# Three products of a gated linear attention, cut into two row tiles of 64 rows that share two PSUM banks

## The chip, the cores and the metric

The kernel runs on one core of a Trainium2 chip. The metric is the device time of one execution in microseconds (us); the time before is the median of three runs. A core has five engines that work at the same time and meet through semaphores: TensorE (PE, matrix products; PEld is its loading of the stationary operand), VectorE (DVE), ScalarE (ACT), GpSimd (POOL) and SyncE (SP, which issues the transfers). Products land in PSUM, in eight banks of 128 partitions by 512 fp32 columns.

## The reference

Two layers of a decoder trunk on a sequence of 256 tokens of width 1024. Each layer normalises x, projects it, runs three groups of heads and projects back. Groups A (causal attention, 8 heads) and M (attention into 256 memory tokens, 4 heads) are left out of this cut; group B is the chunked gated linear attention (GLA), with 4 heads, key width 32, value width 64:

```python
for l in range(DEPTH):                                   # DEPTH = 2
    h = rms_norm(x, g_pre[l]);  u = h @ w_in[l]          # split into the inputs of groups A, B and M
    log_a = log_sigmoid(rb @ w_gate_up[l] + b_gate_up[l]) / 16
    ob = gla_attention(qb * 32 ** -0.5, kb, vb, log_a)   # 4 heads, chunks of 64 tokens
    ob = rms_norm(ob, g_gla_out[l]) * silu(gb)
    x = x + concat([oa, ob, om]) @ w_out[l]
# gla_attention, written over the whole sequence, b = cumsum(log_a):
# att[i, j] = sum_d q[i, d] * k[j, d] * exp(b[i, d] - b[j, d])   for j <= i;   out = att @ v
```

## The kernel before

The kernel is one instruction stream per engine. The order on each engine is not written by hand: generators describe the work as steps (engine, estimated cost, ready time, priority), and a planner (`Plan`, L48 to L128) picks the next step by its own estimates. Steps of PE carry a mode, the shape of the part of the array that they use ("full", "64", "64r", "32"); the planner holds a step of another mode back a little and charges a change of mode. When an estimate or a mode changes, all later steps may be placed otherwise. The engines then follow that fixed order, each waiting on semaphores where an operand or a buffer is not ready.

PE's main work are the projections, as three fp32r products each (high and low parts): L1000 (256 or 272 columns) and L1007 (two weight blocks side by side, 512 columns). ACT and DVE split the weights into the parts (whi at L406, wlo at L408), evacuate PSUM and do the softmax; POOL does powers (cc at L484) and scalings. Head norms of q and k go L471 (squares, ACT), L475 and L482 (sums ss, DVE), L484 (cc, POOL), L491 (nh, DVE), and then L504 (transposes of nh, PE).

GLA builds its 256 by 256 decayed products in pieces of causal blocks, for all four heads at once: the heads' 32 key rows are stacked on the 128 partitions, and the moving operand (z, or qbd for the diagonal) holds a copy of the queries for each head that is zero outside that head's rows. So one product over 128 rows gives four heads' columns. The pieces, in `gla` (L640):

- far (L681): the second half of the queries against the first half of the keys, one product of 128 by 512 columns into a bank of its own, evacuated into `rect` as one copy of 512 columns;
- neighbour (L688): within each half, the second chunk of 64 against the first, two products on 64 columns of the array each, 256 columns, copied into `ad` as two copies of 64 partitions by 256;
- diagonal (L694): eight blocks of 32 by 32, products on 32 columns of the array, 128 columns, added into `acc` where a mask says so (L705, one instruction of 256 columns);
- the levels between (level_mms, L616 and L623), three in a first call, three in a second, in banks of their own.

These operands are fp32, so that every one of these products shows as two MATMUL instructions in the trace, each half of the time. Copies go through a helper (L258 and L260 ACT, L264 and L266 DVE), by the planner's choice of engine. At the end L734 multiplies the assembled matrix with the values.

Of the kernel before, what the change touches and what calls it, by code (L numbers as in the profile page):

```python
# [16 lines left out]
P = 128  # L17
# [25 lines left out]
C_DIAG = 128 + 80  # L43
# [125 lines left out]
def trunk(ctx, tc, xp_d, w0_d, memT_d, wvr_d, win_d, wmkv_d, wout_d, wup_d, cst_d, nb_d, out_d):  # L169
# [4 lines left out]
    V, S, G, TE = nc.vector, nc.scalar, nc.gpsimd, nc.tensor  # L174
# [26 lines left out]
    rect = att[:, 2]  # L201
    ad = att[:, 0:2].rearrange("p g h t -> p (g h) t")
# [33 lines left out]
    def op(eng, cost, after=0.0, prio=None, table=None, mode="full"):  # L236
        return ("op", [(eng, cost)], after, prio, table, mode)

    def tiled(cost, after, prio=None, mode="64"):
        return op("P", cost, after, prio, None, mode)  # L240

    def vcost(n, rate=1.04):
        return 65 + rate * n
# [7 lines left out]
    def copy(dst, src, n, psum, after, prio=None, scale=None, alts="SV"):  # L251
        costs = {"S": scost(n, psum, 0 if scale is None else 1),
                 "V": vcost(n, 1.04 if psum else 0.52) + (0 if scale is None else 60),
                 "G": gcost(n, True)}
        eng, t = yield ("op", [(e, costs[e]) for e in alts], after, prio, None, "full")
        if eng == "S":
            if scale is None:
                S.activation(dst, src, AF.Copy)  # L258
            else:
                S.activation(dst, src, AF.Copy, scale=scale)  # L260
        elif eng == "G":
            G.tensor_scalar(dst, src, 1.0 if scale is None else scale, 1.0, op0=ALU.mult, op1=ALU.mult)
        elif scale is None:
            V.tensor_copy(dst, src)  # L264
        else:
            V.tensor_scalar(dst, src, scale, None, op0=ALU.mult)  # L266
        return t
# [372 lines left out]
    def gla(l, tq, tk, tb):  # L640
# [35 lines left out]
        ta = yield ("wait", lv[0])  # L676
        z = zs.data[0][2]
        bk, t0 = yield ("acq", banks, 3)
        b7, b6, bl = (x[2] for x in bk)
        t = yield op("P", 860, max(tz, t3, t0))  # L680
        TE.matmul(b7, lhsT=ee[:, 0:2], rhs=z[:, :, 0:P], start=True, stop=True)  # L681
        trect = yield from copy(rect, b7.rearrange("p (h t) -> p h t", h=4), 512, True, t)
        banks.release(bk[0:1], trect)
        p6 = b6[:, :256].rearrange("p (a t) -> p a t", t=64)
        pd = b6[:, 256:512].rearrange("p (g h t) -> p g h t", g=2, h=4)
        t = yield tiled(427, max(tz, t3, t0))
        for g in range(2):
            TE.matmul(p6[64 * g:64 * g + 64], lhsT=ee[:, 2 + g], rhs=z[:, :, P + 64 * g:P + 64 * g + 64],  # L688
                      start=True, stop=True)
        zlp.release(zs.data, t)  # L690
        t = yield tiled(427, max(tq, tk, t0), None, "32")
        for m in range(8):
            c = m % 4
            TE.matmul(pd[32 * c:32 * c + 32, m // 4], lhsT=kf[:, 32 * m:32 * m + 32],  # L694
                      rhs=qbd[:, :, 32 * m:32 * m + 32], start=True, stop=True)
        es, zz = lv[0].data
        tl = yield tiled(870, max(ta, t0), None, "32")
        level_mms(0, es[0][2], zz[0][2], bl)
        elp.release(es, tl)
        zlp.release(zz, tl)  # L700
        t1 = yield from copy(ad[0:64, 0:4, 64:128], p6[0:64], 256, True, t)
        t2 = yield from copy(ad[0:64, 4:8, 64:128], p6[64:128], 256, True, t)
        t64 = max(t1, t2)
        td = yield op("V", vcost(256), t)
        V.copy_predicated(acc, msk[:, None, C_DIAG:C_DIAG + 32].to_broadcast([P, 8, 32]),  # L705
                          pd.rearrange("p g h t -> p (g h) t"))
        banks.release(bk[1:2], max(t64, td))
        for o in (0, 64):
            t32 = yield from copy(ad[o:o + 32, :, o + 32:o + 64],
                                  bl[o:o + 32, :256].rearrange("p (a t) -> p a t", t=32), 256, True, tl)  # L710
# [546 lines left out]
```

## Time and profile before

| | |
|---|---|
| time, median of 3 runs | 278.67 us (278.08 to 278.72) |
| the profiled execution | 279.74 us, span 278.0 us from the first to the last instruction |
| PE | 271.7 us busy, 98% of the span |
| DVE, ACT, POOL | 228.3, 192.6 and 92.6 us busy |
| mean granted TensorE clock | 1.000 |

The span is what the trace shows; the profiled execution's time is 1.7 us longer, for start and end. Layer 0 takes about the first 144 us and layer 1 the rest. The ends of matmuls in the trace are modelled, so distances between starts tell how long PE was taken: in a run of L1007 the starts are 0.23 us apart, while each is shown 0.39 us long.

### The profile page before, as it was taken

What the parts mean: (1) busy time and instruction counts of PE and PEld (TensorE: products, weight loads), DVE (VectorE), ACT (ScalarE), POOL (GpSimd) and SP (SyncE); (2) the same over time, 40 slices, a digit from 0 to 9 for tenths busy, and PEclk for the clock granted to TensorE, in tenths of its full rate; (3) what the DMA queues carried; (4) which work ended last, traced back from release to release, by engine and by line L of the source; (5) the groups of instructions that cost most, each with busy time, mean ns of one, the idle gap of its engine ahead of it and who ended that gap; (6) DMA issues with size and microseconds to landing.
All of it is one profiled execution on the core that took longest, in us unless ns stands there. A gap on an engine that the chain in (4) does not pass through costs nothing.

```text
span 278.0 us, 5780 instructions
## 1 busy us (share of the span) xinstructions
PE 271.7 (98%) x2140; PEld 241.6 (87%) x2140; DVE 228.3 (82%) x571; ACT 192.6 (69%) x429; POOL 92.6 (33%) x109
## 2 busy tenths in 40 slices
PE   8999999989999999999999999999999999999994
PEld 6998887768998998999999886789888788999994
DVE  3999999979897998978899698978797777898621
ACT  5849895856768867958774878756987764976400
POOL 3422285680543470600053408213234630420000
PEclk9999999999999999999999999999999999999999
DMA  6999618270743152444454645228142516160111
GB/s 208 389 371 356 223 20 323 114 295 7 290 166 103 51 185 121 154 155 151 158 167 164 277 152 202 104 77 322 58 153 92 211 45 261 20 252 34 57 57 40
DMA packets 8556, 45.76 MB, mean 165 GB/s; under 512 B 960, under 2 KB 2384, under 8 KB 3536
## 3 DMA queue, kind: packets, MB, share of 16 engines
q1 hardware_dynamic: 8528, 45.39, 44.7%
q8 instruction: 17, 0.28, 0.4%
q14 instruction: 11, 0.09, 0.1%
HBM read 44.34 MB, written 1.05 MB: 163 GB/s over the span
## 4 chain that ended last, share of the span: by engine, by line
PE 78%; DVE 11%; DMA 4%; POOL 2%; ACT 1%; issue 1%; SPq 1%; POOLq 0%
PE bank L1000 45%; PE bank L1007 17%; DVE wlo L408 4%; PE bank L949 4%; PE bank L934 3%; PE bank L882 3%; DMA raw<-memT_dram 3%; PE bank L504 2%; DMA raw<-w_dram 2%; POOL cc L484 1%; PE bank L734 1%; DVE ol L302 1%; DVE sqs L318 1%; DVE ss L475 1%; ACT pe L899 1%
## 5 line engine op out<-in xcount | busy, mean ns | idle before, releaser
L408 DVE TENSOR_TENSOR wlo<-raw,whi 128x512 fp32r<-128x512 f32 (+1 forms) x144 | 97.9, 703 | 13.2 <-ACT whi L406 11.8
L406 ACT ACTIVATE whi<-raw 128x512 fp32r<-128x512 f32 (+1 forms) x144 | 86.2, 624 | 21.8 <-PE bank L1000 7.9
L1000 PE MATMUL bank<-xh,whi 128*128 128x256 f32 x160 | 46.5, 291 | 0.0
L1000 PE MATMUL bank<-xl,whi 128*128 128x256 f32 x160 | 44.6, 279 | 0.0
L1000 PE MATMUL bank<-xh,wlo 128*128 128x256 f32 x160 | 44.6, 279 | 0.0
L919 POOL TENSOR_SCALAR pe<-pe,rc 128x256 f32<-128x256 f32 (+1 forms) x48 | 29.4, 626 | 39.1 <-DVE rc L916 37.6
L1000 PE MATMUL bank<-oh,whi 128*128 128x256 f32 x128 | 36.2, 282 | 0.0
L1000 PE MATMUL bank<-oh,wlo 128*128 128x256 f32 x128 | 36.0, 281 | 0.0
L1000 PE MATMUL bank<-ol,whi 128*128 128x256 f32 x128 | 36.0, 281 | 0.0
L484 POOL TENSOR_TENSOR cc<-ss,nhalf 128x8 f32<-128x8 f32 x12 | 21.5, 1800 | 40.4 <-DVE ss L482 40.4
L1007 PE MATMUL bank<-whi,xh 128*128 128x512 f32 x80 | 33.4, 418 | 0.0
L1000 PEld LDWEIGHTS bank<-xh,whi 128*128 128x128 f32 x160 | 30.2, 189 | 1.6 <-issue 1.4
L1007 PE MATMUL bank<-wlo,xh 128*128 128x512 f32 x80 | 31.4, 392 | 0.0
L1007 PE MATMUL bank<-whi,xl 128*128 128x512 f32 x80 | 31.3, 392 | 0.0
L1000 PEld LDWEIGHTS bank<-xl,whi 128*128 128x128 f32 x160 | 30.1, 188 | 0.1
L1000 PEld LDWEIGHTS bank<-xh,wlo 128*128 128x128 f32 x160 | 30.2, 189 | 0.0
L1000 PE MATMUL bank<-whi,xh 128*128 128x256 f32 (+1 forms) x96 | 28.2, 294 | 0.0
L1000 PE MATMUL bank<-wlo,xh 128*128 128x256 f32 (+1 forms) x96 | 27.4, 285 | 0.3 <-DVE wlo L349 0.3
L1000 PE MATMUL bank<-whi,xl 128*128 128x256 f32 (+1 forms) x96 | 27.0, 282 | 0.0
L1000 PEld LDWEIGHTS bank<-oh,wlo 128*128 128x128 f32 x128 | 24.6, 192 | 0.0
L1000 PEld LDWEIGHTS bank<-oh,whi 128*128 128x128 f32 x128 | 24.0, 188 | 0.2 <-issue 0.2
L1000 PEld LDWEIGHTS bank<-ol,whi 128*128 128x128 f32 x128 | 24.0, 188 | 0.0
(188 smaller groups left out, 609.3 us busy)
## 6 DMA issues: line engine op xcount, KB each, us to landing
raw<-win_dram SPq DMA_DIRECT2D x23, 1024.0 KB, 5.1
raw<-wout_dram SPq DMA_DIRECT2D x8, 1024.0 KB, 4.9
raw<-wmkv_dram SPq DMA_DIRECT2D x4, 1024.0 KB, 4.9
raw<-memT_dram SPq DMA_DIRECT2D x2, 1024.0 KB, 6.1
raw<-wvr_dram SPq DMA_DIRECT2D x1, 1088.0 KB, 5.1
raw<-w_dram SPq DMA_DIRECT2D x4, 264.0 KB, 4.5
raw<-w_dram SPq DMA_DIRECT2D x2, 528.0 KB, 7.1
nb<-nb_dram SPq DMA_DIRECT2D x1, 1024.0 KB, 9.2
```

The costliest lines, as they stand in the source:

```text
L302: V.scalar_tensor_tensor(lo[:, k], src[:, k], col(l, g0 + k), hi[:, k].bitcast(F32), op0=ALU.mult, op1=ALU.subtract)
L318: V.tensor_tensor(sqs, sqs, sq[:, j], op=ALU.add)
L406: S.activation(hi[:, cs], raw[:, cs], AF.Copy)
L408: V.tensor_sub(lo[:, cs], raw[:, cs], hi[:, cs].bitcast(F32))
L484: G.tensor_tensor(c, ss, nhalf, op=ALU.pow)
L504: TE.transpose(ps[:, m, tt * P:tt * P + P], n[:, tt, m * P:m * P + P], ident)
L882: TE.matmul(bk[hh][2][:, a:b], lhsT=x[ds], rhs=y[ds], start=(j == 0), stop=(j == len(prs) - 1))
L919: G.tensor_scalar(pe[:, hh, a:b], pe[:, hh, a:b], rc[:, hh, qt:qt + 1], 1.0, op0=ALU.mult, op1=ALU.mult)
L934: TE.transpose(bk[0][2][:, dst:dst + P], pe[:, hh, src:src + P], ident)
L949: TE.matmul(po[64 * hh:64 * hh + 64, q0:T], lhsT=vv[:, j, c:c + 64], rhs=pt[:, hh, 256 * j:256 * j + T - q0], start=(j == 0), stop=(j == 1))
L1000: TE.matmul(ps, lhsT=a, rhs=b, start=(first and j == 0), stop=(lastk and j == 2))
L1007: TE.matmul(ps, lhsT=a, rhs=b, start=(first and j == 0), stop=(lastk and j == 2))
```

## The change

The far, neighbour and diagonal products are each cut into two products over 64 rows (one pair of heads each, j = 0 and 1), with half the columns. Rows 0 to 63 of the operands go to one half of the array's rows and write the bank bx[0], rows 64 to 127 to the other half and write bx[1]. All three pieces lie in these two banks (columns 0 to 255 far, 256 to 383 neighbour, 384 to 511 diagonal), where far had a bank of its own before and the other two shared one. Far and neighbour are now one step of PE, with mode "64r" and an estimate of 640 ns; the diagonal is its own step with 230. The copies double: two of 256 columns for far, four of 128 for neighbour, two masked ones of 128 for the diagonal. Line numbers behind the change are 13 higher in the new kernel (L1007 is L1020, L705 is L718); far is L685, neighbour L689, the diagonal L702.

```diff
-        b7, b6, bl = (x[2] for x in bk)
-        t = yield op("P", 860, max(tz, t3, t0))
-        TE.matmul(b7, lhsT=ee[:, 0:2], rhs=z[:, :, 0:P], start=True, stop=True)
-        trect = yield from copy(rect, b7.rearrange("p (h t) -> p h t", h=4), 512, True, t)
-        banks.release(bk[0:1], trect)
-        p6 = b6[:, :256].rearrange("p (a t) -> p a t", t=64)
-        pd = b6[:, 256:512].rearrange("p (g h t) -> p g h t", g=2, h=4)
-        t = yield tiled(427, max(tz, t3, t0))
+        bx, bl = [x[2] for x in bk[:2]], bk[2][2]
+        p6 = [x[:, 256:384].rearrange("p (a t) -> p a t", t=64) for x in bx]
+        pd = [x[:, 384:512].rearrange("p (g h t) -> p g h t", g=2, h=2) for x in bx]
+        t = yield tiled(640, max(tz, t3, t0), None, "64r")
+        for j in range(2):
+            r = slice(64 * j, 64 * j + 64)
+            TE.matmul(bx[j][:, 0:256], lhsT=ee[r, 0:2], rhs=z[r, 2 * j:2 * j + 2, 0:P], start=True, stop=True)
         for g in range(2):
-            TE.matmul(p6[64 * g:64 * g + 64], lhsT=ee[:, 2 + g], rhs=z[:, :, P + 64 * g:P + 64 * g + 64],
-                      start=True, stop=True)
+            for j in range(2):
+                r = slice(64 * j, 64 * j + 64)
+                TE.matmul(p6[j][64 * g:64 * g + 64], lhsT=ee[r, 2 + g],
+                          rhs=z[r, 2 * j:2 * j + 2, P + 64 * g:P + 64 * g + 64], start=True, stop=True)
         zlp.release(zs.data, t)
-        t = yield tiled(427, max(tq, tk, t0), None, "32")
+        trect = 0
+        for j in range(2):
+            t1 = yield from copy(rect[:, 2 * j:2 * j + 2], bx[j][:, 0:256].rearrange("p (h t) -> p h t", h=2),
+                                 256, True, t)
+            trect = max(trect, t1)
+        td = yield tiled(230, max(tq, tk, t0), None, "32")
         for m in range(8):
             c = m % 4
-            TE.matmul(pd[32 * c:32 * c + 32, m // 4], lhsT=kf[:, 32 * m:32 * m + 32],
-                      rhs=qbd[:, :, 32 * m:32 * m + 32], start=True, stop=True)
+            for j in range(2):
+                r = slice(64 * j, 64 * j + 64)
+                TE.matmul(pd[j][32 * c:32 * c + 32, m // 4], lhsT=kf[r, 32 * m:32 * m + 32],
+                          rhs=qbd[r, 2 * j:2 * j + 2, 32 * m:32 * m + 32], start=True, stop=True)
...
-        t1 = yield from copy(ad[0:64, 0:4, 64:128], p6[0:64], 256, True, t)
-        t2 = yield from copy(ad[0:64, 4:8, 64:128], p6[64:128], 256, True, t)
...
-        banks.release(bk[1:2], max(t64, td))
+        for j in range(2):
+            for g in range(2):
+                t1 = yield from copy(ad[0:64, 4 * g + 2 * j:4 * g + 2 * j + 2, 64:128], p6[j][64 * g:64 * g + 64],
+                                     128, True, t)
...
+        for j in range(2):
+            td = yield op("V", vcost(128), td)
+            V.copy_predicated(ac[:, :, 2 * j:2 * j + 2],
+                              msk[:, None, None, C_DIAG:C_DIAG + 32].to_broadcast([P, 2, 2, 32]), pd[j])
+        banks.release(bk[0:2], max(t64, td, trect))
```

How the planner places this on PE is seen in layer 1, before:

```order
L681 MATMUL bank_97<-zl_136,ee 128x512
L1007 MATMUL bank_94<-whi,xh 128x512
L1007 MATMUL bank_94<-wlo,xh 128x512
L1007 MATMUL bank_94<-whi,xl 128x512
L688 MATMUL bank_93<-zl_136,ee 64x256 x2
L694 MATMUL bank_93<-qbd,kf 32x128 x8
L616 MATMUL bank_99<-zl_135,el_131 32x128 x4
```

The same place in the changed kernel, from the second half of far on, with the semaphores that an instruction waits for (Activation is ACT, Pool POOL); of the 16 diagonal products, which alternate between the two banks, the first two stand here, and the levels L616 and L623 follow them:

```order
L685 MATMUL bank_97<-zl_136,ee 128x256 [waits Pool_49]
L689 MATMUL bank_95<-zl_136,ee 64x128 [waits DVE_49]
L689 MATMUL bank_97<-zl_136,ee 64x128
L689 MATMUL bank_95<-zl_136,ee 64x128
L689 MATMUL bank_97<-zl_136,ee 64x128
L1020 MATMUL bank_92<-whi,xh 128x512
L1020 MATMUL bank_92<-wlo,xh 128x512
L1020 MATMUL bank_92<-whi,xl 128x512
L702 MATMUL bank_95<-qbd,kf 32x64 [waits Activation_49]
L702 MATMUL bank_97<-qbd,kf 32x64 [waits DVE_49]
```

Neighbour now follows far at once, the diagonal opens the second tiled group, and it waits for the two copies of far's result (one on ACT, one on DVE in layer 1; both on ACT in layer 0, with six instead of three L1020 ahead). In layer 0 the steps behind it move too. On DVE there, before (att are the copies of neighbour and of a level, wz and el level operands, ss the sums of the head norms):

```order
L264 COPY att<-bank_95 64x4x64
L705 COPY_PREDICATED acc<-cst,bank_95 128x256
L595 TENSOR_TENSOR wz_133<-el_132,qf 128x128
L264 COPY att<-bank_97 32x8x32
L595 TENSOR_TENSOR wz_133<-el_132,qf 128x128
L635 COPY_PREDICATED acc<-cst,bank_97 128x8x16
L595 TENSOR_TENSOR wz_133<-el_132,qf 128x128
L635 COPY_PREDICATED acc<-cst,bank_97 128x16x8
L603 TENSOR_TENSOR el_132<-el_132,kf 128x32x4
L408 TENSOR_TENSOR wlo<-raw,whi 128x512 x2
L475 TENSOR_REDUCE ss_694<-sq_104 128x8
```

In the changed kernel, from the same point on:

```order
L264 COPY att<-bank_94 64x2x64
L408 TENSOR_TENSOR wlo<-raw,whi 128x512 x3
L264 COPY att<-bank_94 64x2x64
L475 TENSOR_REDUCE ss_693<-sq_104 128x8
L475 TENSOR_REDUCE ss_699<-sq_103 128x8
L482 TENSOR_TENSOR ss_693<-ss_693,evx_320 128x8
L595 TENSOR_TENSOR wz_133<-el_132,qf 128x128
L482 TENSOR_TENSOR ss_699<-ss_699,evx_320 128x8
L718 COPY_PREDICATED acc<-cst,bank_94 128x2x64
```

The sums of the head norms moved ahead of the masked adds and of the level operands. Later in layer 0, PE's products L949 (group A's probabilities by values) and L882 (group M's logits), which alternated in four groups before (8 MATMULs of L949 in the trace, 12 of L882, and again), stand as one group of 24 of L882 and one of L949. Behind layer 0, PE's order is as before but for the GLA pieces and the next L504, which stands six instead of three L1020 behind the levels.

## Rows read from the trace of the kernel before

**Rows 1.** The page: busy time by engine, and the granted clock in 40 slices.

```profile
PE 271.7 (98%) x2140; PEld 241.6 (87%) x2140; DVE 228.3 (82%) x571; ACT 192.6 (69%) x429; POOL 92.6 (33%) x109
...
PEclk9999999999999999999999999999999999999999
```

**Rows 2.** Waits of PE: waiting line <- releaser: us in total, times, longest.

```profile
PE bank L504 <- DVE nh L491: 0.8, 2, 0.6
```

**Rows 3.** Timeline of PE, layer 0, the first head-norm transposes: start us, shown length, instruction.

```profile
60.98 0.40 PE L1007 MATMUL bank<-whi,ol 128*128 128x512 f32 x1
61.94 0.33 PE L504 MATMUL bank<-cst,nh 128*128 128x128 f32 x1 [0.56 <-DVE nh L491]
62.47 0.55 PE L504 MATMUL bank<-cst,nh 128*128 128x128 f32 x3 [0.20 <-DVE nh L491]
62.77 0.48 PE L1007 MATMUL bank<-whi,oh 128*128 128x512 f32 x1
```

**Rows 4.** Timeline of PE, layer 1, around GLA's first products.

```profile
170.54 0.39 PE L1007 MATMUL bank<-whi,xl 128*128 128x512 f32 x1
170.76 1.10 PE L681 MATMUL bank<-zl,ee 128*128 128x512 f32 x2
...
172.16 0.40 PE L1007 MATMUL bank<-whi,xl 128*128 128x512 f32 x1
172.49 0.65 PE L688 MATMUL bank<-zl,ee 128*64 128x256 f32 x4
173.07 0.65 PE L694 MATMUL bank<-qbd,kf 128*32 128x128 f32 x16
173.53 0.49 PE L616 MATMUL bank<-zl,el 128*32 128x128 f32 x5
...
174.52 0.51 PE L1007 MATMUL bank<-whi,xh 128*128 128x512 f32 x1
174.86 0.40 PE L1007 MATMUL bank<-wlo,xh 128*128 128x512 f32 x1
```

**Rows 5.** Timeline of PE, layer 0, far's product.

```profile
47.90 1.02 PE L681 MATMUL bank<-zl,ee 128*128 128x512 f32 x2
```

**Rows 6.** Timeline of PE, layer 1, products over 64 rows in two row halves.

```profile
197.35 0.72 PE L882 MATMUL bank<-kfT,qfT 64*128 64x128 f32 x8
197.82 0.37 PE L882 MATMUL bank<-kh,qh 64*128 64x256 f32 x2
```

**Rows 7.** Timeline of PE, window 180.690 to 180.715 us alone.

```profile
180.69 0.26 PE L623 MATMUL bank<-zl,el 128*32 128x64 f32 x4
```

**Rows 8.** ACT: timeline of layer 0, and a group by form (count, busy, mean ns).

```profile
49.12 1.14 ACT L406 ACTIVATE whi<-raw 128x512 fp32r<-128x512 f32 x2
...
L471 ACT ACTIVATE sq<-bank 128x256 f32<-128x256 f32 x16 | 5.4, 373 | 1.9 <-PE bank L1007 1.8
```

**Rows 9.** DVE: timeline of layer 1, and a group by form.

```profile
172.27 0.28 DVE L585 TENSOR_TENSOR el<-b 128x128 f32<-128x128 f32 x1
174.27 0.42 DVE L491 TENSOR_TENSOR nh<-bank,cc 128x256 f32<-128x256 f32 x1
...
L460 DVE COPY R<-bank 128x256 f32<-128x256 f32 x2 | 0.8, 418 | 0.2 <-PE bank L457 0.2
```

**Rows 10.** The chain that ended last, layer 0: start us, us, what.

```profile
51.80 0.60 DVE wlo L408
...
56.97 1.19 DVE ss L475 x2
...
58.32 3.12 POOL cc L484
```

**Rows 11.** The chain that ended last, groups M and A in layer 0.

```profile
88.14 0.80 PE bank L949 x8
88.94 0.91 PE bank L882 x12
...
118.73 1.45 PE bank L949 x16
```

More of the change, by code (lines that the diff above doesn't have):

```diff
@@ L700, in gla @@
         zlp.release(zz, tl)
-        t1 = yield from copy(ad[0:64, 0:4, 64:128], p6[0:64], 256, True, t)
-        t2 = yield from copy(ad[0:64, 4:8, 64:128], p6[64:128], 256, True, t)
[L703 to L706, printed above, removed]
-        banks.release(bk[1:2], max(t64, td))
+        t64 = t
+        for j in range(2):
+            for g in range(2):
+                t1 = yield from copy(ad[0:64, 4 * g + 2 * j:4 * g + 2 * j + 2, 64:128], p6[j][64 * g:64 * g + 64],
+                                     128, True, t)
+                t64 = max(t64, t1)
+        ac = acc.rearrange("p (g h) t -> p g h t", g=2)
+        for j in range(2):
[3 more added lines that the diff above has]
+        banks.release(bk[0:2], max(t64, td, trect))
         for o in (0, 64):
```

## The prediction

> **What bounds the kernel now.** I read the page first. PE is busy in 98% of the span, and the granted clock stands at its upper level in all 40 slices [rows 1]. Busy matmuls say little by themselves, since their ends are modelled, so I went through PE's timeline and compared distances between starts: 0.23 us in a run of L1007. Next I read PE's waits. After the start-up the largest entry is L504, which waits for nh on DVE [rows 2], and the timeline shows where: in layer 0, near 61 us [rows 3]. The last L1007 starts at 60.98 and is through at 61.21; L504 starts at 61.94, 0.73 late, and its second product 0.53 behind the first where 0.11 is the pace, another 0.42. PE stands for 1.15 us there. So PE's work is the bound nearly everywhere: work that PE saves shows in the time one to one, a new wait of PE costs one to one, and DVE, ACT and POOL count only where PE waits for them.
>
> **The products themselves.** The place to price is layer 1 [rows 4]. From 170.77 (L1007 at 170.54 and its 0.23) to the second L1007 behind the levels at 174.86 there are 4.09 us, with four L1007 of 0.23 in them: 3.17 us of GLA. Its parts: far 0.86 by layer 0's pace, where the next L1007 is held back accordingly [rows 5]; neighbour 172.49 to 173.07, 0.58; diagonal to 173.53, 0.46. Into a tiled group costs 0.10 (172.16 to 172.49 is 0.33 and not 0.23). Out of one costs about 0.22: 174.52 to 174.86 is 0.11 over the pace, and I take as much before it.
>
> What half the rows and half the columns do is shown by L882, which already works on 64 rows in pairs [rows 6]: eight MATMULs of 128 columns take 0.47 us. Far's 0.43 for each MATMUL of 512 columns makes 0.107 for 128; eight in a row would be 0.86, four pairs side by side 0.43. So pairs run side by side. The first round is late by some 0.10 (0.47 less 0.43, and what the first pair needs before the second starts; this is an estimate).
>
> - Far: 0.43, with the first round 0.53 (bounds 0.43 and, with no overlap, 0.86).
> - Neighbour: four tiles at once, 0.21, and 0.10 for the change of tile shape that 0.58 against 0.43 shows today: 0.31 (0.21 to 0.86).
> - Diagonal: 32 MATMULs of half the columns of today's 16. With eight tiles at once 0.23; with issue at today's 0.46/16 = 29 ns each it would be 0.92. The nearest row is L623, products of the same 64 columns: four start inside a window of 25 ns [rows 7], about 7 ns apart, so 32 need some 0.22. I take 0.25, and 0.10 for the change of shape to the levels.
> - The levels stay: 173.53 to 174.52 and 0.11, 1.10.
> - Far becomes tiled, so there is one more pair of in (0.10) and out (0.20 to 0.22).
>
> Sum: 0.10 + 0.53 + 0.31 + 0.20 for the first group, 0.10 + 0.25 + 0.10 + 1.10 for the second, 2.69 against 3.17. I take 0.45 saved in a layer, **0.9 us in both**. This is little, because the second way in and out takes back 0.3.
>
> The Trainium skill, "TensorEngine Tiling (Array Packing)", Instruction Overhead, says that a matmul costs about 60 cycles however few columns it has, and warns against tiling a dimension that is small already. At 2.4 GHz that is an estimate of 25 ns, 0.80 us for the diagonal and 1.1 us more over both layers. The trace disagrees with it for tiles side by side, by the four starts in 25 ns.
>
> **The new wait.** The diagonal now writes banks that ACT and DVE still read, and the order shows L702 waiting for both copies of far. In layer 0 both stand on ACT. PE starts far at 47.90 [rows 5]; with 1.15 for the group, six L1007 (1.38) and 0.10, L702 could start at 50.5. ACT has L406 at 49.12 [rows 8], the first copy at 49.64, another L406 and then the second copy. L406 takes 0.52 from start to start (1.14 for two, each 0.62), a copy of 256 columns like L471's 0.37, with the next 0.29 behind its start. The second copy ends at 49.64 + 0.29 + 0.52 + 0.37 = 50.82. With 0.06 for the semaphore, **0.35 lost**. In layer 1 the second copy is DVE's, behind L585 at 172.27 [rows 9], so 172.47 to 172.89; PE would be ready at 170.77 + 1.14 + 3 x 0.23 = 172.60. **0.3 lost.** Bounds: none where the queues run early, one L406 (0.52) or L408 (0.60) more each where they run late. What stands behind L702 on PE is everything: levels, projections. So the products' 0.9 shrinks to 0.25.
>
> On DVE in layer 1 four small copies wait for L702 (to about 173.4) and stand ahead of both L491, the second of which starts at 174.27 today [rows 9] and would end near 175.85. L504 moved back by three L1007, to about 175.77: **0.1 to 0.15 lost** (0 to 0.6).
>
> The added copies (six instructions a layer, at some 0.2 to 0.3) are about 0.8 us of ACT and DVE. They are hidden as long as PE is the bound; uncovered they would cost that much.
>
> **What moves in layer 0.** The head-norm sums L475 start at 56.97, 5.17 us behind the L408 at 51.80 [rows 10], after the masked adds and level operands that the order shows there. In the new order that L408 comes one place earlier, at about 51.1, and only four L408 (0.60 each) and two small copies (0.2) lead from there to the sums: L475 near 53.9, cc near 55.3 and, with the 3.12 that this first cc takes, done near 58.4. DVE comes to L491 at about 58.0, so nh is whole near 59.2. PE's next L504 stands behind 30 L1007, which begin at 50.85 + 0.25 + 0.10 + 1.10 = 52.3, so at 59.2. Its wait of 1.15 would go; I take **1.0**, since both sides meet within 0.1 (0 to 1.15).
>
> Later in layer 0, L949, L882, L949, L882 [rows 11] take 0.80 + 0.91 + 0.80 + 0.91 = 3.42. As one group of 24 L882 (12 pairs at 0.12 and 0.20 for the first, 1.6) and 16 L949 (1.45 as the same row group shows) they take 3.05: **0.4 saved** (0 to 0.5).
>
> **Sum.** -0.9 + 0.65 + 0.15 - 1.0 - 0.4 = -1.5 us. The profiled execution took 279.74 us, 0.4% over the median; its span of 278.0 becomes 276.5, and the median 278.67 - 1.5 = **277.2 us**.
>
> **The rivals.**
> - The wait of L504 stays (18%). cc's 3.12 us is one reading, and DVE's and ACT's queues ahead of L491 are estimates that meet PE within 0.1 us. Then layer 0 gains nothing up to 62 us, layer 1 nets zero, and the 0.4 of the merged groups is left: 278.3, no measurable change.
> - The copies come later than I read them (10%): one more L406 in layer 0 and L408 in layer 1 ahead of them, 1.1 more: 278.3. For it speaks that ACT and DVE have little idle time there; against it, that the order puts one instruction between the result and the later copy. The Trainium skill says the like in the same page, PSUM Bottleneck: tiling speeds up TensorE and not the evacuation, which can become the bound; the wait in the order agrees, no run here shows its length yet.
> - The diagonal is bound by issue (9%): 0.92 for 0.25, 1.35 in both layers: 278.5. By the page's 25 ns it would be 278.3.
> - The row halves do not run side by side (7%), so the same columns pass twice: far 0.86, neighbour 0.86, diagonal 0.92, together 1.55 more a layer: 280.3, slower. L882 speaks against it, where the halves also write two banks. It turns the result to slower from 1.2 us more in a layer on.
>
> **The numbers.** Under 0.3% (0.84 us) a measurement of this kernel hardly tells from no change. Faster is the forecast alone, 56%, with a range of its own from 276.4 (all of its terms at their good end without the copies' wait would be near 276) to 277.8. Within 0.3% lie the first three rivals, 37%; slower is the last, 7%. To leave out no more than 2 in 10, the range must take in the first three: 276.4 to 278.6.
>
> **What would show it.** Right: L685 and L689 as one group of about 1.1 us; the 32 MATMULs of L702 within 0.3; a stop of PE of 0.3 to 0.4 ahead of L702 in either layer, put down to ACT's and DVE's copies; no stop ahead of L504 in layer 0; one L882 group of 24. Wrong: a gap ahead of L504 near 60 us that is still about 1 us; L702 at 0.9; a copy of far that ends more than 0.5 behind PE; new stops of PE in the attention part of layer 0, where the order changed most and which I priced at nothing.

## The result, and the profile after

The changed kernel takes 276.6 us (median of 6 runs, 276.46 to 277.49; the kernel before on the same chip 278.7). The ratio is 0.9911, with a 95% interval of 0.9889 to 0.9933: 2.5 us less (278.67 x 0.0089), where I forecast 1.5. The direction was right, the size was not: by the ratio the time is 276.2, just below my range. The two profiled executions differ by more, 278.0 against 274.9 us of span.

The page after (busy time, the granted clock in 40 slices), which answers to [rows 1]:

```profile
PE 269.3 (98%) x2184; PEld 240.0 (87%) x2184; DVE 226.5 (82%) x573; ACT 195.2 (71%) x437; POOL 88.6 (32%) x107
...
PEclk9999999999999999999999999999999999999999
```

PE is still the bound, at the same clock. Its timeline at the places of [rows 4, 5], GLA's products in layer 0, and then, as in [rows 3], the first head-norm transposes:

```profile
47.70 0.40 PE L1020 MATMUL bank<-whi,xl 128*128 128x512 f32 x1
48.02 0.70 PE L685 MATMUL bank<-zl,ee 64*128 64x256 f32 x4
48.66 0.45 PE L689 MATMUL bank<-zl,ee 64*64 64x128 f32 x8
49.04 0.50 PE L1020 MATMUL bank<-whi,xh 128*128 128x512 f32 x1
...
50.30 0.39 PE L1020 MATMUL bank<-whi,xl 128*128 128x512 f32 x1
50.62 0.70 PE L702 MATMUL bank<-qbd,kf 64*32 64x64 f32 x32
51.24 0.51 PE L616 MATMUL bank<-zl,el 128*32 128x128 f32 x5
...
52.59 0.40 PE L1020 MATMUL bank<-wlo,oh 128*128 128x512 f32 x1
...
59.01 0.39 PE L1020 MATMUL bank<-whi,ol 128*128 128x512 f32 x1
59.24 0.60 PE L504 MATMUL bank<-cst,nh 128*128 128x128 f32 x4
59.59 0.48 PE L1020 MATMUL bank<-whi,oh 128*128 128x512 f32 x1
```

From the end of the L1020 at 47.70 (its 0.23 gives 47.93) to 52.59 there are 4.66 us with seven L1020 of 0.23 in them, so 3.05 us of GLA. The same count in the kernel before (47.90 to its second L1007 behind the levels at 51.93, less four) gives 3.11. GLA brought 0.06 us here, its new wait included, where I had 0.10 (0.45 less 0.35). At 59.24 L504 follows its predecessor by 0.23: the stop of [rows 3] is not there. In layer 1 the timeline shows a new stop, shorter than that one:

```profile
167.22 0.39 PE L1020 MATMUL bank<-whi,xl 128*128 128x512 f32 x1
167.54 0.70 PE L685 MATMUL bank<-zl,ee 64*128 64x256 f32 x4
168.18 0.45 PE L689 MATMUL bank<-zl,ee 64*64 64x128 f32 x8
...
169.46 0.62 PE L702 MATMUL bank<-qbd,kf 64*32 64x64 f32 x32
170.01 0.51 PE L616 MATMUL bank<-zl,el 128*32 128x128 f32 x5
...
171.35 0.39 PE L1020 MATMUL bank<-wlo,xh 128*128 128x512 f32 x1
...
172.53 0.33 PE L504 MATMUL bank<-cst,nh 128*128 128x128 f32 x1
173.06 0.55 PE L504 MATMUL bank<-cst,nh 128*128 128x128 f32 x3 [0.20 <-DVE nh L491]
173.36 0.48 PE L1020 MATMUL bank<-whi,xh 128*128 128x512 f32 x1
```

GLA takes 2.98 us (167.45 to 171.35, less four L1020) for 3.17; L504 then needs 0.83 up to the next L1020, where four such transposes without a wait take 0.35 (59.24 to 59.59).

What I had nothing for stands in the windows. Of the kernel before and then of the changed one: us, PE busy and its instructions (those that reach in from the edges counted), granted clock, DMA share, GB/s.

```profile
97.20:148.30 51.10, 51.10 (x443) 1.00 0.48 166
124.60:138.60 14.00, 14.00 (x122) 1.00 0.49 168
250.00:270.00 20.00, 20.00 (x172) 1.00 0.13 47
```

```profile
95.00:145.00 50.00, 50.00 (x443) 1.00 0.47 168
122.60:136.60 14.00, 14.00 (x126) 1.00 0.46 174
250.00:270.00 20.00, 20.00 (x172) 1.00 0.12 42
```

The same 443 instructions take 51.1 us in one trace and 50.0 in the other, with no wait of PE for another engine in the view of waits there and the full clock in both. In the 14 us of layer 0's output projection 126 MATMULs fit instead of 122: the starts of L1000 (L1013) with 256 columns lie 117.8 ns apart in one and 113.3 in the other. Both paces occur in each trace; they hold over dozens of products and change where the stream changes: where another instruction or a stop comes between, or where the operands change sides. At 91.66 us of the changed kernel's trace, `whi,xh` becomes `xh,whi` in L1013 with nothing between, and 117.8 becomes 113.3 within three products. In the last 20 us both kernels run at 117.8.

### The profile page after: what moved, and what is told of

Same layout as the page of the kernel before. It is cut to its first block, busy times and chain, and to the rows that moved or that the text cites. A ratio compares the mean times of both kernels' runs of the same rounds, so it can differ in the third digit from the quotient of the medians.

```text
span 274.9 us, 5873 instructions
## 1 busy us (share of the span) xinstructions
PE 269.3 (98%) x2184; PEld 240.0 (87%) x2184; DVE 226.5 (82%) x573; ACT 195.2 (71%) x437; POOL 88.6 (32%) x107
## 3 DMA queue, kind: packets, MB, share of 16 engines
HBM read 44.34 MB, written 1.05 MB: 165 GB/s over the span
## 4 chain that ended last, share of the span: by engine, by line
PE 86%; DVE 5%; DMA 4%; issue 1%; POOL 1%; SPq 1%; ACT 1%; POOLq 0%; DVEq 0%
PE bank L1013 48%; PE bank L1020 21%; PE bank L962 4%; PE bank L947 3%; PE bank L895 3%; DMA raw<-memT_dram 2%; PE bank L504 2%; DMA xp<-xp_dram 2%; DVE wlo L408 1%; POOL oh L262 1%; PE bank L747 1%; DVE sqs L318 1%; DVE ol L302 1%; PE bank L623 1%; PE bank L702 0%
## 5 line engine op out<-in xcount | busy, mean ns | idle before, releaser
L408 DVE TENSOR_TENSOR wlo<-raw,whi 128x512 fp32r<-128x512 f32 (+1 forms) x144 | 97.4, 699 | 13.5 <-ACT whi L406 12.1
L1013 PE MATMUL bank<-xh,whi 128*128 128x256 f32 x160 | 46.3, 289 | 0.0
L1013 PE MATMUL bank<-xl,whi 128*128 128x256 f32 x160 | 44.5, 278 | 0.0
L1013 PE MATMUL bank<-xh,wlo 128*128 128x256 f32 x160 | 44.5, 278 | 0.0
L932 POOL TENSOR_SCALAR pe<-pe,rc 128x256 f32<-128x256 f32 (+1 forms) x48 | 27.3, 583 | 39.9 <-DVE rc L929 27.0
L1013 PE MATMUL bank<-oh,whi 128*128 128x256 f32 x128 | 35.9, 280 | 0.0
L1013 PE MATMUL bank<-ol,whi 128*128 128x256 f32 x128 | 35.8, 280 | 0.0
L1013 PE MATMUL bank<-oh,wlo 128*128 128x256 f32 x128 | 35.7, 279 | 0.0
L484 POOL TENSOR_TENSOR cc<-ss,nhalf 128x8 f32<-128x8 f32 x12 | 20.9, 1746 | 42.0 <-DVE ss L482 35.2
L1020 PE MATMUL bank<-whi,xh 128*128 128x512 f32 x80 | 32.7, 409 | 0.0
L1013 PEld LDWEIGHTS bank<-xh,whi 128*128 128x128 f32 x160 | 30.1, 188 | 1.6 <-issue 1.4
L1020 PE MATMUL bank<-wlo,xh 128*128 128x512 f32 x80 | 31.4, 393 | 0.0
L1020 PE MATMUL bank<-whi,xl 128*128 128x512 f32 x80 | 31.3, 391 | 0.0
L1013 PEld LDWEIGHTS bank<-xl,whi 128*128 128x128 f32 x160 | 30.1, 188 | 0.1
L1013 PEld LDWEIGHTS bank<-xh,wlo 128*128 128x128 f32 x160 | 30.2, 189 | 0.0
L1013 PE MATMUL bank<-whi,xh 128*128 128x256 f32 (+1 forms) x96 | 28.1, 293 | 0.0
L1013 PE MATMUL bank<-wlo,xh 128*128 128x256 f32 (+1 forms) x96 | 27.6, 287 | 0.4 <-DVE wlo L349 0.3
L1013 PE MATMUL bank<-whi,xl 128*128 128x256 f32 (+1 forms) x96 | 27.1, 282 | 0.0
L1013 PEld LDWEIGHTS bank<-oh,wlo 128*128 128x128 f32 x128 | 24.3, 190 | 0.0
L1013 PEld LDWEIGHTS bank<-oh,whi 128*128 128x128 f32 x128 | 24.0, 188 | 0.2 <-issue 0.2
L1013 PEld LDWEIGHTS bank<-ol,whi 128*128 128x128 f32 x128 | 24.0, 188 | 0.1
```

Source lines behind the costliest of these rows:

```text
L408: V.tensor_sub(lo[:, cs], raw[:, cs], hi[:, cs].bitcast(F32))
L484: G.tensor_tensor(c, ss, nhalf, op=ALU.pow)
L932: G.tensor_scalar(pe[:, hh, a:b], pe[:, hh, a:b], rc[:, hh, qt:qt + 1], 1.0, op0=ALU.mult, op1=ALU.mult)
L1013: TE.matmul(ps, lhsT=a, rhs=b, start=(first and j == 0), stop=(lastk and j == 2))
L1020: TE.matmul(ps, lhsT=a, rhs=b, start=(first and j == 0), stop=(lastk and j == 2))
```

## The experiments

All ratios are against the kernel before, with 95% intervals; the changed kernel has 0.9911.

**Each kernel once more.** No edit.

> The kernel before, unchanged, in a second profiled execution. In its first one the 443 matmuls between 97.2 and 148.3 us took 51.10 us, and the same work of the changed kernel 50.0; the L1000 start 117.8 ns apart there against 113.3. If the order of the instructions decides on the pace (A), the same stretch takes 51.0 to 51.2 again and the execution 279.4 to 279.9 us. If the pace is a matter of the single execution (B), it comes out anywhere from 50.0 to 51.1, and the execution between 277.9 and 279.8 us, as the six times of this kernel lie.

> The changed kernel, unchanged, in a second profiled execution. Pace by the order (A): the stretch from 95 to 145 us takes 50.0 us again, 276.7 in all. Pace by the execution (B): up to 1.1 us more in that stretch, 276.5 to 277.8 in all; then about 1.1 of the 3.1 us between the two first profiles says nothing of the change.

The kernel before took 277.96 us (span 276.2), the changed one 276.08 (274.3). In the changed kernel both traces show the same pace nearly everywhere. In the kernel before, the second execution has no stop ahead of L504: POOL's first cc (L484) took 1.67 us, not the 3.1 of the first. Its source view, and the timeline:

```profile
L484 POOL TENSOR_TENSOR cc<-ss,nhalf x2: 1633/1651/1669, 58.0 to 59.7; 128x8 f32<-128x8 f32 x2
```

```profile
60.77 0.39 PE L1007 MATMUL bank<-whi,ol 128*128 128x512 f32 x1
61.00 0.60 PE L504 MATMUL bank<-cst,nh 128*128 128x128 f32 x4
61.36 0.48 PE L1007 MATMUL bank<-whi,oh 128*128 128x512 f32 x1
```

And from 124.6 to 138.6 us it holds 126 MATMULs:

```profile
124.60:138.60 14.00, 14.00 (x126) 1.00 0.42 151
```

So the same program, instruction for instruction, has the stop or has it not (1.15 us), and has the slow or the fast pace there; B is right for the kernel before. But this second execution is a fast one: its 277.96 us lie below all eleven other times of the kernel on that chip (278.63 to 280.01), so most executions pay a part of these losses.

Two smaller stops are in both traces of the kernel before and in neither of the changed one. The second call of the levels waits within its group for el, and L749, the second of a pair of products (L748, L749; L761 and L762 behind the change), waits for qsl. Before, and then after:

```profile
58.68 1.12 PE L623 MATMUL bank<-zl,el 128*32 128x64 f32 x48
59.73 0.50 PE L1007 MATMUL bank<-whi,oh 128*128 128x512 f32 x1
...
80.93 0.19 PEld L749 LDWEIGHTS bank<-qsl,blk 128*128 128x128 f32 x1 [0.34 <-DVE qsl L746]
```

```profile
60.47 0.88 PE L623 MATMUL bank<-zl,el 128*32 128x64 f32 x48
61.27 0.50 PE L1020 MATMUL bank<-whi,oh 128*128 128x512 f32 x1
```

The levels take 1.05 us there (1.11 in the second trace) and 0.80 after the change. The two pairs of L748 and L749 in layer 0 take 0.88 us up to the next starts (1.06 in the second trace) and 0.48 after it. Together these stops cost 0.65 and 0.88 us.

**Order alone, tiles alone.** One kernel has the order of the changed one on every engine with the old products in its places, the other the old order with the tiles:

```diff
# order alone, in gla of the changed kernel
+        TE.matmul(bx[0], lhsT=ee[:, 0:2], rhs=z[:, :, 0:P], start=True, stop=True)
+            TE.matmul(p6[64 * g:64 * g + 64], lhsT=ee[:, 2 + g], rhs=z[:, :, P + 64 * g:P + 64 * g + 64], ...)
...
+            TE.matmul(pd[32 * c:32 * c + 32, m // 4], lhsT=kf[:, 32 * m:32 * m + 32], rhs=qbd[:, :, 32 * m:32 * m + 32], ...)
# tiles alone, in gla of the kernel before: its estimates stay
         t = yield op("P", 860, max(tz, t3, t0))
+        for j in range(2):
+            r = slice(64 * j, 64 * j + 64)
+            TE.matmul(bx[j][:, 0:256], lhsT=ee[r, 0:2], rhs=z[r, 2 * j:2 * j + 2, 0:P], start=True, stop=True)
```

> The order of the changed kernel, instruction by instruction on every engine, but with the products of the kernel before in its places: far as one product of 512 columns, the neighbours of 256, the diagonal of 128, all on 128 rows. If the change of order brings the gain (my reading of the two traces: products 0.06 in layer 0 and 0.2 in layer 1, all else from the order), it is 2.0 to 2.5 us under the kernel before, within 0.5 us of the changed one, and L504 does not wait near 60 us. If the tiles bring it, it stays within 0.5 us of the kernel before.

> The tiles of the changed kernel in the order of the kernel before: the same sequence on every engine, each full product replaced by its row tiles, each copy by its halves. If the order brings the gain (A), this is no faster than the kernel before. By the lengths read in the changed kernel (0.64 far, 0.38 neighbour, 0.55 diagonal, 1.12 levels, 0.09 in) a layer takes 2.78 us for 3.11 to 3.17, 0.7 saved in both; but far and diagonal now follow each other directly, so L702 must wait for far's two copies, 0.5 to 1.0 in a layer: +0.3 to +1.3 us over the kernel before, with the L504 wait near 61 us as there. If the tiles bring the gain (B), it lies 1.5 to 2.5 us under the kernel before.

Order alone: 277.46 us, ratio 0.9933 (0.9914 to 0.9951), 1.9 us less. Tiles alone: 278.87, ratio 0.9988 (0.9979 to 0.9997), 0.3 less, where I had expected 0.3 to 1.3 more. Three quarters of the gain come without a single row tile; L504 is on time in layer 0 (59.32, 0.23 behind the L1020 ahead of it), and the two smaller stops are gone (0.81 and 0.47 us). The other 0.6 are the tiles in the new order: GLA takes 3.32 and 3.38 us with the old products in it, 3.05 and 2.98 with the tiles. In the old order the shared banks bring the wait that I feared, at the neighbour's product in layer 0:

```profile
50.31 0.71 PE L694 MATMUL bank<-zl,ee 64*64 64x128 f32 x8 [0.98 <-ACT att L689]
50.95 0.45 PE L702 MATMUL bank<-qbd,kf 64*32 64x64 f32 x32
51.34 0.52 PE L616 MATMUL bank<-zl,el 128*32 128x128 f32 x5
```

(L694 and L689 are its lines of the neighbour's product and of far's copies.) In layer 1, with the same three L1020 between, no product waits, since ACT comes to the copies earlier, and GLA takes 2.80 us (170.13 to 173.85, less four L1020) for 3.17. The 0.3 us of this run are not the tiles' worth alone: by the 0.98 that PE loses in layer 0 the stops behind it become shorter (no wait at L504 near 61 us, the levels 0.81). In the new order the neighbour's product follows far before any copy reads the banks, and six L1020 (three in layer 1) stand ahead of the diagonal; what is left of the wait is read below. The diagonal, already inside its group and not waiting, takes 0.39 here, change to the levels included. From 124.6 to 138.6 us this kernel holds 121 MATMULs, the order-alone kernel 126 from 122.6 to 136.6.

**The diagonal.** Each of its products twice; and, in the order of the changed kernel, on 128 rows.

```diff
-        for m in range(8):
+        for m in list(range(8)) * 2:                      # twice
...
-            for j in range(2):                            # on 128 rows, one bank for each g
-                r = slice(64 * j, 64 * j + 64)
-                TE.matmul(pd[j][32 * c:32 * c + 32, m // 4], lhsT=kf[r, 32 * m:32 * m + 32], ...)
+            TE.matmul(pd[m // 4][32 * c:32 * c + 32], lhsT=kf[:, 32 * m:32 * m + 32], rhs=qbd[:, :, 32 * m:32 * m + 32], ...)
```

> The changed kernel with every product of the diagonal (L702) issued twice, into the same place. If the group of 32 MATMULs takes its 0.55 to 0.62 us because each costs some 17 to 19 ns to issue (C), 64 take 1.1 to 1.2, and the kernel loses 1.1 us over both layers. If 32 take 0.25, as I forecast, and the rest is a wait for the copies of far that the weight loads hide (D), 64 take 0.80 to 0.87, and it loses 0.5 us.

> The changed kernel, in exactly its order, with the diagonal alone as eight products on 128 rows (16 MATMULs of 128 columns) as in the kernel before, each half in one of the two shared banks. If L702 takes its 0.55 to 0.62 us because of its number of small products (C), this group takes the 0.46 us of before, and the kernel is 0.2 to 0.3 us faster than the changed one. If L702 is held by the copies of far (D), the group still takes 0.55 to 0.62 or starts that much later, and the time is unchanged.

Twice (277.05 us, 0.9924, 0.9901 to 0.9946), in layers 0 and 1:

```profile
50.17 1.09 PE L702 MATMUL bank<-qbd,kf 64*32 64x64 f32 x64
51.19 0.52 PE L616 MATMUL bank<-zl,el 128*32 128x128 f32 x5
...
169.34 0.95 PE L702 MATMUL bank<-qbd,kf 64*32 64x64 f32 x64
170.22 0.52 PE L616 MATMUL bank<-zl,el 128*32 128x128 f32 x5
```

64 take 1.02 and 0.88 us where 32 took 0.62 and 0.55: 32 more cost 0.40 and 0.33, between C and D. The starts of the single MATMULs in the changed kernel settle it. First, in either layer, the later of far's two copies, and what PE has started of L702 by 0.05 us behind that copy's end (windows 50.60 to 50.86 and 169.45 to 169.62 us). Then the run of the tiles in the old order, where all 32 start in a window of 0.25 us (172.11 to 172.36):

```profile
50.45 0.36 ACT L258 ACTIVATE att<-bank 128x256 f32<-128x256 f32 x1
50.62 0.30 PE L702 MATMUL bank<-qbd,kf 64*32 64x64 f32 x2
169.16 0.41 DVE L264 COPY att<-bank 128x256 f32<-128x256 f32 x1
169.46 0.30 PE L702 MATMUL bank<-qbd,kf 64*32 64x64 f32 x2
```

```profile
172.12 0.45 PE L702 MATMUL bank<-qbd,kf 64*32 64x64 f32 x32
```

Two MATMULs, the first product, have started by then. The third, the first to write the bank of the later copy, starts at 50.86 and 169.63, 0.05 to 0.06 behind that copy's end. From it to the last are 0.24 us, 8 ns from start to start, and 0.15 more to L616. So in this kernel 32 take what I forecast. The rest of the 0.62 and 0.55 is a wait for the copy (D), 0.16 and 0.08, and 0.08 between the first two starts, which no run here explains. With the products twice, the first 32 stand 8 ns apart as well; only the second 32, into the same places, take about 0.39 us, 12 ns each.

On 128 rows the group takes 0.49 and 0.46 (L700 at 50.64 to L616 at 51.13; 169.63 to 170.09). That is the time that C named, but it does not speak for C: in this edit the second bank is first written by the fifth product, at 50.89, when the copy is done anyway. The kernel is no faster: 0.9916 (0.9902 to 0.9930). Its trace gains 0.15 us on the changed one at the diagonal of layer 0 and has lost it at 63 us, where L504 takes longer. It is 0.34 ahead from 83 us on, since its products from 70 to 77 us go at 113.3 ns for 117.8. It falls 0.17 behind at layer 1's statistics, where DVE waits 0.90 for whi at 142.7, and ends 0.05 ahead. The diagonal's gain, 0.1% of the time, can't be told from that.

**The pace.** Small extra products at six places of layer 1's output projection; then one transpose ahead of it; then two on the kernel before.

```diff
+                    if (l, g, m) in ((1, 0, 0),) and k == KORD[l][0]:      # before: ((0, 1, 0), (1, 0, 0))
+                        TE.transpose(ps[:, 0:P], ident, ident)
                     mms(ps, l, "f", w, (oh, ol), k, m, k == KORD[l][0], k == KORD[l][-1])
```

> The changed kernel, with a small extra product ahead of each of the six last half groups of the output projection of layer 1 (24 MATMULs of 256 columns each, all at 117.8 ns from start to start so far): a transpose, an fp32r product of 128 columns, two of 256, one of 64 rows, four of 32 columns, two of 64 columns. If the pace is a state that an interruption leaves behind and that holds to the next one (C), some of the six turn 117.8 into 113.3 for the 24 MATMULs behind them, each such piece 0.11 us shorter. If the pace belongs to the place (the banks, the operands, the weights in memory) (D), all six pieces stay at 117.8. The extra products cost 0.1 to 0.4 us each.

> The changed kernel with one extra transpose of 128 x 128 ahead of the output projection of layer 1, near 247 us, into a bank that the next product overwrites. If PE's pace is a state (C), the 192 MATMULs behind it run at 113.3 ns for 117.8: 0.86 us less, 0.11 for the transpose, 0.75 in all: 275.8 us or 1.2% under the kernel before. If the pace does not hold, or something else than PE sets the end (D), the time is that of the changed kernel or 0.1 more.

> The kernel before, without tiles or new order, with two such transposes: one ahead of the second group of the output projection of layer 0 (144 MATMULs behind it) and one ahead of that of layer 1 (192). If the pace is a state that any kernel can set (C): 0.75 less behind the second; behind the first 0.54 less in executions that stood at 117.8 there and 0.1 more in those at 113.3: 0.7 to 1.3 us under the kernel before, and in the profile the stretch from 122 to 142 us at 113.3. Then the drift of 1.1 us between the two first profiles has nothing to do with row tiles. If it hangs on the tiles or on the order (D), no change.

The six pieces, mean distance of starts from the third product on, worked out from the trace: 117.8 ns ahead of the first, then 114.2 behind the transpose, 114.4 (fp32r of 128 columns), 117.8 (two of 256), 113.5 (64 rows), 113.6 (32 columns), 113.5 (64 columns). C is right: with the same operands the pace is what the interruption leaves, and two products of the same width turn it from fast to slow. One transpose in the changed kernel: 275.63 us, 0.9872 (0.9852 to 0.9892), 1.0 us less than the changed kernel by the medians. Its trace gains 0.7 us behind the transpose. Another 0.36 lie far ahead of it: from 70 to 77 us, where the instructions on every engine are the same, it goes at 113.3 ns and the two traces of the changed kernel at 117.8. Two in the kernel before: 278.41, 0.9968 (0.9952 to 0.9983), 0.9 us less with nothing else changed. The windows of the changed kernel with one, then of the kernel before with two:

```profile
250.00:270.00 20.00, 20.00 (x177) 1.00 0.13 47
```

```profile
124.60:138.60 14.00, 14.00 (x126) 1.00 0.41 152
250.00:270.00 20.00, 20.00 (x178) 1.00 0.12 41
```

172 became 177 and 178. So the drift of 1.1 us between my first two traces is a pace of PE that a kernel of either kind can have.

**Layer 1's transposes, and sums of steps.** The four small copies of layer 1 on ACT; that with the transpose; the diagonal on 128 rows with both and two more transposes in layer 0 and layer 1; and far held back until the levels are ready.

```diff
-                t1 = yield from copy(ad[...], p6[j][64 * g:64 * g + 64], 128, True, t)
+                t1 = yield from copy(ad[...], p6[j][64 * g:64 * g + 64], 128, True, t, alts="SS" if l else "SV")
...
-        t = yield tiled(640, max(tz, t3, t0), None, "64r")
+        t = yield tiled(640, max(tz, t3, t0, ta), None, "64r")      # far held back, with the diagonal on 128 rows
```

> The changed kernel, with the four small copies of the neighbour's products in layer 1 given to ACT alone; on PE the order stays, on DVE L491 moves ahead of the place of the four copies. If these copies on DVE (1.19 us ahead of L491) make L504 late in layer 1, 0.49 us by the comparison with the kernel before, that stop near 172.5 us goes, and the kernel is 0.4 to 0.5 us faster than the changed one: 276.1 us. If L504 is late for another reason (the cc of POOL, or nothing but the row before it), it stays late and the time within 0.1.

> The changed kernel with the small copies of layer 1 on ACT and the one transpose ahead of the output projection of layer 1. If the two steps add (0.49 and 0.61 in their profiles), it lies 1.1 us under the changed kernel: 275.0 to 275.4 us, 1.4 to 1.5% under the kernel before. If the pace is thrown by the first step, 276.0.

> The changed kernel with the diagonal on 128 rows, the small copies of layer 1 on ACT, and three transposes (ahead of the second half of qm in layer 0, of qm in layer 1, of the output projection of layer 1). Sum of the steps as read so far: 0.25 + 0.45 + 0.75, and 0.1 to 0.3 each from the first two transposes if the pace holds over the short groups that follow: 1.5 to 1.9 us under the changed kernel, 274.7 to 275.1 us, 1.4 to 1.6% under the kernel before. If the steps don't add, 275.5 or more.

> The changed kernel with two edits: far and neighbour wait in the plan for the operands of the levels, so that they stand closer to the second group, and the diagonal is eight products on 128 rows again, of 128 columns, one bank for each half of them. Where all is one group, a layer's products take 0.09 + 0.64 + 0.38 + 0.46 + 1.12 = 2.69 us for 2.99 to 3.05 in the changed kernel, 0.6 to 0.7 less in both; where the groups stay apart only the diagonal's 0.1 to 0.15 a layer. The order moves with it, so the waits of L504 can come or go: 275.3 to 276.3 without a new one, 276.6 to 277.5 with one near 1 us.

Copies on ACT: 276.13 us, 0.9897 (0.9875 to 0.9919), and L504 is on time:

```profile
171.86 0.60 PE L504 MATMUL bank<-cst,nh 128*128 128x128 f32 x4
172.21 0.48 PE L1020 MATMUL bank<-whi,xh 128*128 128x512 f32 x1
```

0.35 us for the 0.83 of the changed kernel, so the copies on DVE ahead of L491 had cost 0.48. With the transpose the two steps add: 274.89 us, 0.9868 (0.9845 to 0.9892), the fastest version here, 1.7 us under the changed kernel by the medians and 1.2 by the ratios; 0.48 and 0.7 make 1.2, and its profile has the fast pace from 70 to 77 us, too. All steps together gave only 276.01, 0.9889 (0.9869 to 0.9909): the extra transpose in layer 0 met a stretch that stood at 113.3 and left it at 117.8, so it is no switch to the fast pace, and layer 1's statistics cost this trace 0.4 us, as they cost the run with the diagonal on 128 rows 0.5. Far held back: 278.33, 0.9968 (0.9955 to 0.9981), slower than either case that I had expected. The groups did not become one (twelve L1020 stand between them in layer 0), the order moved everywhere behind, and L1020 and L457 wait 0.6 us in new places; where the rest of its loss lies I did not trace.

**The wait of L504, timed by itself.** On the kernel before, two L408 were put behind the two sums L475, alone and with the two transposes. In a first form of the edit the loads overwrote weights before L408 had read them; its times (283.55 and 282.75 us) say nothing. In the mended form:

> The kernel before with one change of order on DVE: the two L408 of layer 0 that stand ahead of the two head-norm sums L475 near 55.4 us come behind them, and the buffers that they read are given back 1.2 us later, so two loads of weights start that much later. The sums end 1.1 us earlier, and L504 near 61 us is no longer late, whether POOL's cc takes 3.1 us or 1.67. If that wait is there in most timed executions (A), the median falls by 0.8 to 1.1 us against the kernel before; if it was a matter of few executions (B), by less than 0.4. If the later loads make PE wait behind 61 us, the profile shows L1007 or L1000 waiting for wlo there.

> The same with the two transposes of the earlier run on the kernel before (0.9 us by that run's ratio). If wait and pace are separate terms that add: 0.9 and what the sums give, 1.3 to 2.0 us under the kernel before. If they are the same executions (an execution that waits loses its pace, too), no more than 0.9 to 1.1.

Both are slower: 281.12 us, 1.0062 (1.0039 to 1.0085), and 280.26, 1.0036 (1.0023 to 1.0049). L482, which closes the sums, still stands behind the two L408, so cc starts at 58.5, no earlier than in the kernel before (58.3); and the later loads make the second pair of L504 wait:

```profile
65.41 0.33 PE L511 MATMUL bank<-cst,nh 128*128 128x128 f32 x1 [0.60 <-DVE nh L498]
66.13 0.55 PE L511 MATMUL bank<-cst,nh 128*128 128x128 f32 x3 [0.39 <-DVE nh L498]
```

(L511 is L504 there.) The edit was no test of the wait, and neither A nor B is decided by it. The transposes take back about 0.9 here, too (281.12 - 280.26), but in the trace only that of layer 1 does: behind that of layer 0 the products stay at 117.8, where the same transpose on the kernel before left 113.3.

## Why the prediction was right and wrong

- **The products**: net right, by luck. I had 0.9 saved and 0.65 lost to the new wait, 0.25 in all; GLA took 0.06 and 0.19 less, 0.25 in all, but by two errors of 0.4 that cancel. Without its waits (0.16 and 0.08 by the starts of L702) GLA saved 0.49: far took 0.64 (forecast 0.53), neighbour 0.38 (0.31), the change of shape behind the diagonal 0.15 (0.10), and I had nothing for the 0.08 between the diagonal's first two starts. The reading of [rows 7] held: 32 MATMULs in 0.24 (0.25). The new wait is there, for the copies that I named, and the later one in layer 0 ended at 50.81, where I had 50.82; it cost 0.24 for 0.65, since PE came to it later. The rival of issue is refuted for these 32, at 8 ns each. The Trainium skill's 60 cycles ("TensorEngine Tiling (Array Packing)", Instruction Overhead), an estimate of 25 ns, is not what these tiles show, neither here nor in the second pass of the run with the products twice (12 ns).
- **L504 in layer 1**: 0.48 for 0.15. The mechanism was the one I named, DVE's four copies ahead of L491; they took 1.19 us in a row, and nh was whole at 173.00, 0.49 behind L504's place (172.51), where I had 0.08 between the two.
- **The wait of L504 in layer 0**: gone, as forecast, but its price, 1.15 us, is paid in one of three traces. In the traces of the old order in which PE comes to L504 on time, cc took 3.1 us once and 1.67 twice. How often it is paid in the timed runs stays open; what makes cc take longer, too.
- **The merged groups**: from 85.97, the first of 24 L895, to L504 at 89.05 are 3.08 us, where I had 3.05 for 3.42. Right, 0.34.
- **The failed step** is "What moves in layer 0": of all that the order moves it counts one wait and one merged group, and takes the other work of PE as unchanged. Two things were not. First, the smaller stops at the levels and at L748 and L749: 0.65, 0.88 and 0.91 us in the three traces of the old order with the old products, and in none of the ten of the new order, where these places take 0.81 and 0.46 to 0.48. Second, the pace of the products behind the merged group. With the new order PE goes at 113.3 ns from 92 to 99 us and from 120 on, in each of ten traces of that order or its near variants. With the old order it goes at 117.8 from 94 to 102 in four of four, and from 120 in three of four (in both traces of the last experiment, too). That is 0.3 us for the first stretch (70 products by 4.5 ns) and 0.8 for the second (by which the two traces of the kernel before differ there). That the pace can change without an edit is shown (same program, both paces); what sets it at 92 us stays open. It isn't the merged group by itself: behind it 18 products still go at 117.8, and the pace turns where the operands change sides.

Added up for my first two traces, in the order of the list: -0.25 (products), +0.48, -1.15, -0.34, then -0.65 for the small stops and -1.1 for the pace make -3.0, of the 3.1 us between their spans. The second pair of traces, without the stop at L504 and without the slow pace from 120 on, differs by 1.9. The 2.5 of the ratio lie between. Of my -1.5, the 1.0 for L504 was one trace's price, and how much of it the timed executions pay stays open; the terms that I missed, 1.0 to 2.0 us, are at least as large as what that can overstate.

Order alone (1.9) and the tiles in that order (0.6) make up the whole. Of the rivals, row halves one after the other, issue, late copies and a lasting stop at L504 are refuted by the rows above.

## What to carry to other kernels

A change that goes through a planner is first a change of order: time the old work in the new order and the new work in the old one before crediting the edit. A wait read in one profile is one execution's; ask for a second profile before it becomes a term of a sum, and add up the small waits as well, for here they were worth 0.65 to 0.9 us. In a group of small products the starts of the single instructions tell a wait from the cost of the products; the length of the group does not. A bank shared between a product and a copy asks for other PE work between the two, enough for the copy's place in its own engine's queue.

## What was not expected of the hardware

PE runs the same stream of 128 x 256 fp32r products at full clock in two paces, 113.3 and 117.8 ns from start to start, 4%. In these traces the pace holds until the stream changes (a transpose, a tiled group, a stop, products with other operands), the same operands show both, and it can differ between two executions of one program. One 128 x 128 transpose at the head of 192 such products was worth 0.7 us in the trace; a transpose at another place left the slow pace as it was once, and once turned the fast one into it. What decides which pace follows is not shown.
